# A two-layer hybrid encoder on one core: the later modulation and second norm held until the gates are done, one modulation tile per part on the tensor engine, three weights not kept in the scratch

## The chip, the core and the metric

The kernel runs on one core of a Trainium2 chip. The metric is the time of one execution on the device, in microseconds (us). The core has a tensor engine (PE, with its weight loads listed as PEld), a vector engine (DVE), a scalar engine (ACT), a general engine (POOL) and a queue engine (SP) that issues all of this kernel's transfers in the order in which they were written. Each engine works through its own list of instructions and waits on semaphores for the others.

## The reference

A sequence of 1024 tokens of width 1024 goes through two layers. Each layer normalizes, modulates with a vector made from the condition `c`, mixes, and adds the gated result to the residual.

```python
cond = jax.nn.silu(c)
for i in range(DEPTH):
    mod = cond @ ada_w[i] + ada_b[i]
    shift, scale, gate = jnp.split(mod[:, None, :], 3, axis=-1)
    h = rmsnorm(x, norm_w[i]) * (1 + scale) + shift
    ...
    x = x + gate * y
return rmsnorm(x, final_norm_w)
```

Layer 0 is a gated DeltaNet: 8 query/key heads and 16 value heads of 128, a causal convolution over four tokens, a decay per head and a triangular inverse per chunk. Layer 1 is softmax attention with a forget gate and 16 heads of 64. The modulation is a product of one row of 1024 numbers with a 1024x3072 matrix per layer: shift, scale and gate are 1024 columns each.

## The kernel before

Layer 0 is computed in two halves of 512 tokens. In each half the input projection is made in eight groups (two value heads each), one 128-column tile after the other: a tile is 24 matmuls of 128x512, because every operand is split into a high and a low part (`split`, L321: ACT casts the high part, DVE or POOL subtracts for the low part) and three products are summed. Group by group the keys are transposed (`tr`), their products are taken (`su`), the triangular blocks are inverted on DVE by 15 small steps (`xtmp`, `xi`, L1065 and L1069), merged on PE (`su<-rmat`), and the state runs through `ch` and `co`. Layer 1 follows from about 1300 us.

The order of PE's instructions is fixed by the kernel itself: a small planner (`Flow`, L87) steps through generators by priority and by estimated PE time. On DVE, ACT, POOL and SP a scheduler of the framework sorts the instructions by its own estimate, so that an edit in one place can move instructions in others.

The parts that the change touches:

- **The first modulation** (`start_norm`, L526). Shift (`scol`) and scale (`gcol`) of layer 0 are the two parts of a loop over `n`. In each, eight tiles of 128x1024 of `ada_w` come in through the buffers `og`, `zg`, `d`, `gb`. Tiles 0 to 5 (`KPE` is 6, L81) are multiplied and summed on DVE (L553, L555) into one tile, also called `d`; PE then sums that tile over its partitions with eight matmuls against `ones`, and takes tiles 6 and 7 with eight matmuls each against `cond`. DVE adds the bias into `scol` or `gcol` (L569). With both, ACT and DVE modulate the normalized x into `ht_h` and `ht_l` (L577 to L582), the moving operands of all projections.
- **The later modulation** (`ada_all`, L1174, which calls `ada_strip`, L257). Layer 0's gate and all of layer 1 are made in 16 strips of 256 columns. A strip has eight loads of 128 KB into three buffers `oraw` (L265) and eight DVE steps into `ohi` (L270, L272), then one or two small matmuls and a copy (`olo`, L299). Three small DVE copies from `scol[0]` into the `oraw` buffers (L1177) make the first loads wait for `scol`.
- **The second norm** (`next_norm`, L607). The tokens of the second half are normalized tile by tile: a load into `nx` (L612), a square sum on ACT into `nh` (L305), a scaling on DVE (L594), transposes and modulation, a store to `h1_d`. Nothing holds the first load of `nx`.
- **The gates** (`gates`, L639) of a half: a short projection, a chain of small DVE steps, the running sum `g_gc` of the log decay, its negative `g_ngc` (L686), and a store `g_d` (L696). From `g_d` each group reads a broadcast `gb` twice through one buffer (`decay`, L831): once for `d1`, which goes into the blocks that are inverted (stored as `lb`, read back as `lr`), once for `d2`. After `gb`, POOL masks (L840) and ACT takes the exponential (L852).
- **The scratch of weights** (`proj_src`, L392, and `proj_tile`, L710). In the first half every projection weight is loaded raw into a `wlo` buffer, split, and both parts are stored to `wc` in DRAM (L719); in the second half the two parts are loaded from there (L398), and nothing is split.

Of the kernel before, what the change touches and what calls it, by code (L numbers as in the profile page):

```python
# [15 lines left out]
P = 128  # L16
D = 1024
S = 1024
KT = D // P
# [58 lines left out]
OGW = 2000  # L78
OL = 4
Y_NN = 8000  # L80
KPE = 6  # L81
Y_GA = 14000
Y_N2 = 6000
ADP = 2000
# [97 lines left out]
def tile_trunk(  # L182
# [24 lines left out]
    nc = tc.nc  # L207
# [7 lines left out]
    def ct(shape, name, dt=F32):  # L215
        return const.tile(shape, dt, name=name, tag=name)
# [31 lines left out]
    scol = [ct([P, KT], f"scol{l}") for l in range(2)]  # L248
# [101 lines left out]
    def xt_(shape, name, bufs=1, dt=F32):  # L350
        return px.tile(shape, dt, name=name, tag=name, bufs=bufs)
# [30 lines left out]
    def wtile(n):  # L382
        hi = xt_([P, D], "whi", 3, F32R)
        if "raw" in where:
            raw = where["raw"].pop(0)
            where["raw"].append(raw)
        else:
            raw = xt_([P, D], "wlo", 5)
        lo = xt_([P, D], "wlo", 5, F32R)
        return hi[:, 0:n], lo[:, 0:n], raw[:, 0:n]  # L390

    def proj_src(src, key, again):  # L392
        def load():
            if again:
                hi = xt_([P, D], "whi", 3, F32R)
                lo = xt_([P, D], "wlo", 5, F32R)
                for v, d in zip((hi, lo), wcache[key]):
                    nc.sync.dma_start(v.bitcast(F32), d)  # L398
                return [tuple(v.rearrange("p (k f) -> p k f", f=P) for v in (hi, lo)) + (None,)]
            hi, lo, raw = (v.rearrange("p (k f) -> p k f", f=P) for v in wtile(D))  # L400
            nc.sync.dma_start(raw, src)
            for c in range(2):
                kc = slice(4 * c, 4 * c + 4)
                later.append(lambda kc=kc: split(hi[:, kc], lo[:, kc], raw[:, kc], lo_eng=nc.vector))
            return [(hi, lo, key)]

        return load

# [82 lines left out]
    with ExitStack() as sa:  # L491
# [3 lines left out]
        def at(shape, name, bufs=1, dt=F32):  # L495
            return pa.tile(shape, dt, name=name, tag=name, bufs=bufs)
# [29 lines left out]
        def start_norm():  # L526
            xsT = [at([P, HALF], n, b) for n, b in (("k", KQ), ("k", KQ), ("k", KQ), ("q", 2), ("q", 2))]
            xsT += [at([P, HALF], "ktok", 3) for _ in range(3)]
            for t in range(CPH):
                xt = at([P, D], *(("vtok", 3), ("qd", 2))[t // 2])  # L530
                nc.sync.dma_start(xt, x[t * P : (t + 1) * P, :])
                for d in norm_tile(xt, at([P, D], "ogt", 1), lambda k, p, t=t: nc.scalar.copy(
                    xsT[k][:, t * P : (t + 1) * P], p)):
                    flow.t += d
            tags = [("d1", 2), ("og", 2), ("zg", ZG), ("d1", 2), ("og", 2), ("zg", ZG), ("gb", 1)]
            cnt = [0]

            def wtag():
                cnt[0] += 1
                return tags[cnt[0] % len(tags)]  # L540

            banks = []
            for _ in range(2):
                banks.append((yield from acc_bank()))
            bcol = at([P, 2, KT], "bcol")
            for n in range(2):
                ps = banks[n]
                acc = at([P, D], "d2", 2)
                for k in range(KT):
                    w = at([P, D], *wtag())  # L550
                    nc.sync.dma_start(w, ada_w[0, k * P : (k + 1) * P, n * D : n * D + D])
                    if k == 0:
                        nc.vector.tensor_scalar(acc, w, cond[:, 0:1], None, op0=ALU.mult)  # L553
                    elif k < KPE:
                        nc.vector.scalar_tensor_tensor(  # L555
                            acc, w, cond[:, k : k + 1], acc, op0=ALU.mult, op1=ALU.add
                        )
                    for s, c, on in ((acc, ones[:, 0:1], k == KPE), (w, cond[:, k : k + 1], k >= KPE)):
                        for j in range(KT if on else 0):
                            mm(  # L560
                                ps[:, j : j + 1], s[:, j * P : (j + 1) * P], c,
                                start=s is acc and j == 0, stop=k == KT - 1 and j == KT - 1,
                            )
                if n == 0:
                    nc.sync.dma_start(bcol, ada_bc)
                    nc.sync.dma_start(norm_c, norm_col)
                    wload()
                    wload()
                nc.vector.tensor_tensor((scol, gcol)[n][0], ps[:, 0:KT], bcol[:, n], op=ALU.add)  # L569
                flow.free(ps, R_AD)  # L570
            nc.vector.scalar_tensor_tensor(
                gcol[0], gcol[0], 1.0, norm_c[:, 0], op0=ALU.add, op1=ALU.mult
            )
            for k in range(KT):
                xk = xsT[k]
                sc, sh = gcol[0][:, k : k + 1], scol[0][:, k : k + 1]
                nc.scalar.activation(ht_h[:, k], xk, AF.Identity, scale=sc, bias=sh)  # L577
                if k % 2:
                    nc.scalar.activation(xk, xk, AF.Identity, scale=sc, bias=sh)
                else:  # L580
                    nc.vector.tensor_scalar(xk, xk, sc, sh, op0=ALU.mult, op1=ALU.add)
                nc.vector.tensor_tensor(ht_l[:, k], xk, ht_h[:, k].bitcast(F32), op=ALU.subtract)  # L582
            nc.sync.dma_start(conv_h, conv_col)
            nc.vector.tensor_scalar(conv_h, conv_h, 0.5, None, op0=ALU.mult)
            nc.sync.dma_start(nw_h, a_nw)
            nc.vector.tensor_scalar(nw_h, nw_h, 0.5, None, op0=ALU.mult)
            nc.sync.dma_start(dt_b, a_dt.broadcast_to([P, 16]))
            nc.sync.dma_start(neg_a, a_log.broadcast_to([P, 16]))
            nc.scalar.activation(neg_a, neg_a, AF.Exp)
            nc.vector.tensor_scalar(neg_a, neg_a, -1.0, None, op0=ALU.mult)  # L590
# [16 lines left out]
        def next_norm():  # L607
            yield from hold(lambda: done["kqv"] >= 2)
            for t in range(CPH):
                tok = CPH * P + t * P  # L610
                xt = at([P, D], "nx", 1)
                nc.sync.dma_start(xt, x[tok : tok + P, :])  # L612
                yield 4000
                hf = at([P, KT, P], "nh", 1)

                def evac(k, p):
                    nc.vector.tensor_scalar(
                        hf[:, k], p, gcol[0][:, k : k + 1], scol[0][:, k : k + 1],
                        op0=ALU.mult, op1=ALU.add,
                    )  # L620

                yield from norm_tile(xt, hf.rearrange("p k t -> p (k t)"), evac)
                yield 3000
                nc.sync.dma_start(
                    h1_d[:, :, t * P : (t + 1) * P].rearrange("k p t -> p k t"), hf
                )
            done["norm"] = 1
# [82 lines left out]
        def proj_tile():  # L710
            hi, lo, key = wnext(2)
            ps = yield from acc_bank()
            for k in range(KT):
                if k == 2 and key is not None:
                    wcache[key] = [
                        dram.tile([P, D], F32, name=f"wc{key}{n}", tag=f"wc{key}{n}") for n in range(2)
                    ]
                    for v, d in zip((hi, lo), wcache[key]):
                        nc.sync.dma_start(d.rearrange("p (k f) -> p k f", f=P), v.bitcast(F32))  # L719
                mm3(ps, hi[:, k], lo[:, k], ht_h[:, k], ht_l[:, k], k == 0, k == KT - 1)  # L720
                if k == 1:
                    wload()
                if k in (3, 5):
                    half()
                if k < KT - 1:
                    yield 0
            return ps
# [446 lines left out]
        def ada_all():  # L1174
            yield from hold(lambda: done["gates"] == 1)
            for _ in range(3):
                nc.vector.tensor_copy(xt_([P, 2 * P], "oraw", 3)[:, 0:KT], scol[0])  # L1177
            for l, cl in strips:
                for w0 in (0, 256):
                    yield from ada_strip(  # L1180
                        xt_, acc_bank, l, cl + w0, 256, ("oraw", 3), ("ohi", 4), ("olo", 4), 1, ADP
                    )

        ts = []
# [634 lines left out]
```

## Time and profile before

| what | value |
|---|---|
| time, median of 3 runs | 2058.69 us (2054.26 to 2058.92) |
| the profiled execution | 2063.72 us, its span 2062.0 us |
| PE, PEld busy | 1853.8 us (90%), 1549.9 us (75%) |
| DVE, ACT, POOL busy | 1364.0, 1033.1, 476.4 us |
| HBM read, written | 235.34 MB, 84.81 MB |
| chain that ended last | PE 57%, DMA 16%, DVE 14% |

In the lines of the profile a group reads "line engine operation out<-in, shapes, count | busy us, mean ns of one | idle time of the engine before them, and what ended it". A row of the timeline has the start, the time until the last of its instructions ends, the engine, the line and the operation; in square brackets stands how long the engine had been idle and who released it. SPq is the time in which the queue engine issues a transfer, not the transfer itself. A table of windows gives each engine's busy time in a stretch, then the granted clock of PE (1.00 is full), the share of the DMA engines and GB/s.

### The profile page before, as it was taken

The page shows a single profiled execution, that of the slowest core. Times are in us where ns is not written, and L with a number is a line of the kernel's source. Part 1 is how long each engine was busy: PE and PEld are TensorE (multiplying, and loading weights), DVE is VectorE, ACT ScalarE, POOL GpSimd, SP SyncE. Part 2 cuts the span into 40 slices and gives each one's busy share as a digit, 9 for nine tenths or more (in the row PEclk, how much of TensorE's full clock was granted, in tenths as well). Part 3 has the DMA queues.
Part 4 walks back from the last instruction along what each step waited for, and adds up shares of the span by engine and source line. Part 5 has one row for each costly group of instructions (what it writes and reads, how often), then busy time and mean ns, then how long its engine had stood idle before and what let it go on. Part 6 is the DMA issues. An engine that isn't in the chain of part 4 may idle for free.

```text
span 2062.0 us, 36440 instructions
## 1 busy us (share of the span) xinstructions
PE 1853.8 (90%) x12972; PEld 1549.9 (75%) x12972; DVE 1364.0 (66%) x3310; ACT 1033.1 (50%) x2678; POOL 476.4 (23%) x518
## 2 busy tenths in 40 slices
PE   5867898988998889989989788999999999999898
PEld 5655676767776677778778566879889889889676
DVE  5867888778767567665666476537656566666664
ACT  3554565554545345554444343336555565555631
POOL 2021221211213122212101231421231331331222
PEclk7888999999999999999999999999999999999999
DMA  8767676667655545454459998310211110111522
GB/s 320 255 194 219 192 248 205 202 211 238 198 164 178 154 133 176 128 177 140 145 172 311 323 317 274 108 53 27 67 45 33 57 57 32 57 59 40 170 84 95
DMA packets 238166, 322.55 MB, mean 156 GB/s; under 512 B 103896, under 2 KB 156656, under 8 KB 237984
## 3 DMA queue, kind: packets, MB, share of 16 engines
q1 hardware_dynamic: 237984, 320.22, 48.4%
q8 instruction: 102, 1.67, 0.3%
q14 instruction: 80, 0.66, 0.1%
HBM read 235.34 MB, written 84.81 MB: 155 GB/s over the span
## 4 chain that ended last, share of the span: by engine, by line
PE 57%; DMA 16%; DVE 14%; ACT 5%; issue 3%; POOL 3%; SPq 2%; DVEq 0%; POOLq 0%; ACTq 0%
PE mm L127 36%; PE lg L127 5%; PE pt L131 3%; PE oT L127 3%; DMA oraw<-in_ada_w_dram 3%; PE su L127 2%; PE tr L131 2%; PE co L127 2%; DMA rmat<-rb 2%; DVE wlo L326 2%; DMA ohi<-og_d 2%; PE ch L127 2%; DVE cv_y L743 1%; DMA gb<-g_d 1%; DVE xtmp L1065 1%
## 5 line engine op out<-in xcount | busy, mean ns | idle before, releaser
L127 PE MATMUL mm<-ht_h,whi 128*128 128x512 f32 x784 | 352.1, 449 | 8.8 <-DVE olo L299 6.2
L127 PE MATMUL mm<-ht_l,whi 128*128 128x512 f32 x784 | 317.2, 405 | 5.7 <-DVE ht_l L582 5.7
L127 PE MATMUL mm<-ht_h,wlo 128*128 128x512 f32 x784 | 317.5, 405 | 0.9 <-POOL wlo L326 0.9
L127 PE MATMUL mm<-whi,h_h 128*128 128x384 f32 x512 | 187.3, 366 | 1.7 <-ACT whi L323 1.7
L127 PEld LDWEIGHTS mm<-ht_h,whi 128*128 128x128 f32 x784 | 155.0, 198 | 40.3 <-DVE olo L299 6.7
L127 PEld LDWEIGHTS mm<-ht_h,wlo 128*128 128x128 f32 x784 | 153.4, 196 | 37.0 <-POOL wlo L326 1.3
L127 PEld LDWEIGHTS mm<-ht_l,whi 128*128 128x128 f32 x784 | 154.9, 198 | 32.6 <-DVE ht_l L582 6.9
L127 PE MATMUL mm<-wlo,h_h 128*128 128x384 f32 x512 | 174.1, 340 | 2.7 <-POOL wlo L326 2.7
L743 DVE SCALAR_TENSOR_TENSOR cv_y<-cv_t,conv_h,cv_y 128x512 f32<-128x512 f32 x192 | 146.5, 764 | 42.7 <-ACT cv_y L735 40.4
L127 PE MATMUL mm<-whi,h_l 128*128 128x384 f32 x512 | 173.6, 339 | 0.0
L1559 DVE TENSOR_TENSOR ptl<-pt,pth 128x512 fp32r<-128x512 f32 x192 | 106.3, 555 | 85.0 <-ACT pth L1558 83.3
L1558 ACT CAST pth<-pt 128x512 fp32r<-128x512 f32 x192 | 91.3, 477 | 130.5 <-PE pt L131 129.4
L1402 POOL TENSOR_TENSOR rs<-ss,mhalf 128x4 f32<-128x4 f32 x64 | 64.5, 1007 | 313.3 <-DVE ss L1400 310.6
L1523 ACT ACTIVATE lg<-lg,mx 128x896 f32<-128x896 f32 (+7 forms) x128 | 99.5, 777 | 54.1 <-DVE mx L1515 49.8
L326 DVE TENSOR_TENSOR wlo<-ht_h,whi 128x512 fp32r<-128x512 f32 x124 | 92.3, 785 | 49.9 <-ACT whi L323 44.0
L323 ACT CAST whi<-ht_h 128x512 fp32r<-128x512 f32 x124 | 70.5, 619 | 91.4 <-DMA ht_h<-in_wa_o_dram 37.4
L127 PEld LDWEIGHTS mm<-wlo,h_h 128*128 128x128 f32 x512 | 97.9, 191 | 6.3 <-POOL wlo L326 4.4
L127 PEld LDWEIGHTS mm<-whi,h_h 128*128 128x128 f32 x512 | 98.5, 192 | 4.4 <-ACT whi L323 2.0
L127 PE MATMUL mm<-h_h,whi 128*128 128x512 f32 x240 | 100.4, 419 | 0.6 <-DVE wlo L1658 0.3
L131 PE MATMUL pt<-ident,lg 128*128 128x128 f32 (+1 forms) x584 | 96.6, 275 | 2.8 <-ACT lg L1523 2.8
L127 PEld LDWEIGHTS mm<-whi,h_l 128*128 128x128 f32 x512 | 97.2, 190 | 0.0
L127 PE MATMUL mm<-h_h,wlo 128*128 128x512 f32 x240 | 94.8, 395 | 0.0
(356 smaller groups left out, 4660.6 us busy)
## 6 DMA issues: line engine op xcount, KB each, us to landing
ht_h<-in_wa_o_dram SPq DMA_DIRECT2D x62, 512.0 KB
wc<-whi SPq DMA_DIRECT2D x48, 512.0 KB
wc<-wlo SPq DMA_DIRECT2D x48, 512.0 KB
wlo<-wc SPq DMA_DIRECT2D x48, 512.0 KB
whi<-wc SPq DMA_DIRECT2D x48, 512.0 KB
wlo<-in_wa_c_dram SPq DMA_DIRECT2D x32, 512.0 KB
oraw<-in_ada_w_dram SPq DMA_DIRECT2D x128, 128.0 KB
gb<-g_d SPq DMA_DIRECT2D x32, 512.0 KB
```

Of the source, the lines that this page charges most:

```text
L127: self.nc.tensor.matmul(out, lhsT, rhs, start=start, stop=stop)
L131: self.nc.tensor.transpose(out, src, ident)
L323: nc.scalar.copy(hi, src)
L326: (lo_eng or nc.gpsimd).tensor_tensor(lo, src, hi.bitcast(F32), op=ALU.subtract)
L743: nc.vector.scalar_tensor_tensor(y, raw[:, j : j + HALF], w[:, j : j + 1], y, op0=ALU.mult, op1=ALU.add)
L1065: nc.vector.tensor_tensor(tv, bc(lr[:, j + 1 :, j], 1, m), xi[:, 0:m, j : j + 1].broadcast_to([P, m, n]), op=ALU.mult,)
L1402: nc.gpsimd.tensor_tensor(rs, ss, mhalf[:, 0:4], op=ALU.pow)
L1523: nc.scalar.activation(lg, lg, AF.Exp, scale=-1.0, bias=mx[:, hh : hh + 1], accum_out=sums[:, tt : tt + 1],)
L1558: nc.scalar.copy(ph_[:, cs], pp[:, cs])
L1559: nc.vector.tensor_tensor(pl_[:, cs], pp[:, cs], ph_[:, cs].bitcast(F32), op=ALU.subtract)
```

## The change

The first tile of the first modulation that goes to PE directly is tile 7 instead of tile 6: DVE sums seven tiles, PE takes the sum and one tile. The loads of the strips and the first load of `nx` are held by small DVE copies from `ngc` of the first half's gates. The three weights with keys 0, 1 and 2 (the key, query and first value tile of group 0) are not stored to the scratch; in the second half they are loaded raw and split again.

```diff
-KPE = 6
+KPE = 7
+KC = 3
...
     def proj_src(src, key, again):
         def load():
-            if again:
+            if again and key >= KC:
...
-            return [(hi, lo, key)]
+            return [(hi, lo, None if again else key)]
...
                             mm(
                                 ps[:, j : j + 1], s[:, j * P : (j + 1) * P], c,
-                                start=s is acc and j == 0, stop=k == KT - 1 and j == KT - 1,
+                                start=s is acc and j == 0, stop=s is w and k == KT - 1 and j == KT - 1,
                             )
...
                 xt = at([P, D], "nx", 1)
+                if t == 0:
+                    nc.vector.tensor_copy(xt[:, 0:KT], ts[0]["gt"]["ngc"][:, 0, 0:KT])
                 nc.sync.dma_start(xt, x[tok : tok + P, :])
...
-                if k == 2 and key is not None:
+                if k == 2 and key is not None and key >= KC:
...
             for _ in range(3):
-                nc.vector.tensor_copy(xt_([P, 2 * P], "oraw", 3)[:, 0:KT], scol[0])
+                nc.vector.tensor_copy(xt_([P, 2 * P], "oraw", 3)[:, 0:KT], ts[0]["gt"]["ngc"][:, 0, 0:KT])
```

PE's list is the same as before but for two sets of eight matmuls (tile 6 of each part), which are gone. The other engines' lists are sorted anew; line numbers of the changed kernel are higher by 1 to 3.

On DVE, right after the scale (`gcol`) is complete, the rows of before are these; `ohi` rows are strips, `ht_l` and the rows with `gcol,scol` make the low part of the modulated x:

```order
L571 SCALAR_TENSOR_TENSOR gcol_88<-gcol_88,norm_c 128x8
L272 SCALAR_TENSOR_TENSOR ohi<-oraw,cond,ohi 128x256 x2
L581 TENSOR_SCALAR k<-k,gcol_88,scol_90 128x512
L272 SCALAR_TENSOR_TENSOR ohi<-oraw,cond,ohi 128x256
L582 TENSOR_TENSOR ht_l<-k,ht_h 128x512
L272 SCALAR_TENSOR_TENSOR ohi<-oraw,cond,ohi 128x256
L581 TENSOR_SCALAR k<-k,gcol_88,scol_90 128x512
L272 SCALAR_TENSOR_TENSOR ohi<-oraw,cond,ohi 128x256
```

In the changed kernel the same place on DVE reads:

```order
L572 SCALAR_TENSOR_TENSOR gcol_88<-gcol_88,norm_c 128x8
L582 TENSOR_SCALAR k<-k,gcol_88,scol_90 128x512
L583 TENSOR_TENSOR ht_l<-k,ht_h 128x512
L582 TENSOR_SCALAR k<-k,gcol_88,scol_90 128x512
L583 TENSOR_TENSOR ht_l<-k,ht_h 128x512
L582 TENSOR_SCALAR q<-q,gcol_88,scol_90 128x512
```

No strip stands between the rows that modulate x any more; the strips begin behind `g_ngc`.

On ACT, at the first group's keys, before has these rows; `sqt` are square sums of the transposed keys and queries, `ktok` is the copy that frees the transposes' bank, `d` with `g_gc` is the exponential of `d1`, `d` with `g_ngc` that of `d2`, which reads the second `gb`:

```order
L898 ACTIVATE sqt,gss<-tr 128x128
L852 ACTIVATE d_757<-d_757,g_gc 128x128 x8
L898 ACTIVATE sqt,gss<-tr 128x128
L747 ACTIVATE cv_t<-cv_y 128x512
L852 ACTIVATE d_872<-d_872,g_ngc 128x128 x3
L928 ACTIVATE gb<-gb 128x512
L852 ACTIVATE d_872<-d_872,g_ngc 128x128
L928 ACTIVATE gb<-gb 128x512
L852 ACTIVATE d_872<-d_872,g_ngc 128x128 x4
L898 ACTIVATE sqt,gss<-tr 128x128 x2
L902 COPY ktok<-tr 128x512
```

The changed kernel has them on ACT in this order:

```order
L901 ACTIVATE sqt,gss<-tr 128x128
L855 ACTIVATE d_731<-d_731,g_gc 128x128 x8
L901 ACTIVATE sqt,gss<-tr 128x128 x3
L905 COPY ktok<-tr 128x512
L750 ACTIVATE cv_t<-cv_y 128x512
L901 ACTIVATE sqt,gss<-tr 128x128 x2
L905 COPY vtok<-tr 128x4x128
L901 ACTIVATE sqt,gss<-tr 128x128 x2
L905 COPY vtok<-tr 128x4x128
L855 ACTIVATE d_846<-d_846,g_ngc 128x128 x3
```

The copy `ktok` has moved from behind the exponentials of `d2` to a place ahead of them.

On SP, from the store of the gates to the reload of the first group's blocks, before has these rows:

```order
L696 DMA g_d<-cv_t 16x512
L401 DMA wlo<-in_wa_z_dram 128x1024
L834 DMA gb<-g_d 128x1024
L719 DMA wc_1190<-whi 128x1024
L719 DMA wc_1191<-wlo 128x1024
L834 DMA gb<-g_d 128x1024
L401 DMA wlo<-in_wa_z_dram 128x1024
L719 DMA wc_1253<-whi 128x1024
L719 DMA wc_1254<-wlo 128x1024
L834 DMA gb<-g_d 128x1024 x2
L1051 DMA lb<-d_757 32x8x32 x4
L1055 DMA lr_890<-lb 32x16x16 x4
```

In the changed kernel SP has, from the same store on, up to the same blocks (`lb`):

```order
L699 DMA g_d<-cv_t 16x512
L615 DMA nx<-in_x_dram 128x1024
L402 DMA wlo<-in_wa_z_dram 128x1024
L266 DMA oraw<-in_ada_w_dram 128x256
L837 DMA gb<-g_d 128x1024
L266 DMA oraw<-in_ada_w_dram 128x256
L722 DMA wc_1164<-whi 128x1024
L722 DMA wc_1165<-wlo 128x1024
L266 DMA oraw<-in_ada_w_dram 128x256 x2
L402 DMA wlo<-in_wa_z_dram 128x1024
L722 DMA wc_1228<-whi 128x1024
L837 DMA gb<-g_d 128x1024
```

Seven strip loads, three of them just ahead of `g_d`, now stand among the gates' transfers up to the second `gb`. Behind it come one more store of a weight, three strip loads, and then `lb`, which no longer stands behind the third and fourth `gb`.

## The prediction

> **What bounds the kernel now.** First the table of windows, to see where PE is short of work.
>
> ```profile
> 0.00:52.00 52.00, 27.83 (x128) 26.00 (x128) 28.46 (x50) 16.77 (x51) 14.35 (x30) 0.70 0.88 320
> 52.00:62.00 10.00, 3.89 (x7) 2.28 (x8) 9.64 (x21) 8.13 (x12) 0.00 (x0) 0.50 0.41 123
> 100.00:130.00 30.00, 14.92 (x78) 11.78 (x76) 11.80 (x31) 22.14 (x73) 14.65 (x17) 0.77 0.51 159
> 130.00:200.00 70.00, 52.52 (x506) 41.80 (x507) 56.27 (x159) 29.49 (x70) 10.29 (x18) 0.87 0.78 243
> 200.00:300.00 100.00, 89.14 (x825) 71.66 (x825) 84.03 (x220) 59.98 (x185) 27.18 (x32) 0.97 0.65 208
> 1300.00:1500.00 200.00, 193.71 (x1115) 170.15 (x1114) 115.56 (x317) 99.32 (x221) 59.85 (x55) 0.98 0.17 53
> ```
>
> The first number behind each stretch is its length, the next PE's busy time. From 1300 us on PE is busy 97%, at 200 to 300 us 89%: there time is PE's work, and a shift made earlier is carried. In the first 62 us PE is busy 31.7 us, from 100 to 200 us 67.4 of 100. The change acts there. Second, PE's waits over the whole span:
>
> ```profile
> PE su L127 <- DMA rmat<-rb: 22.1, 4, 10.3
> PE tr L131 <- ACT ktok L902: 12.5, 1, 12.5
> PE mm L127 <- DVE d L555: 9.7, 2, 6.2
> PE mm L127 <- DVE olo L299: 6.2, 1, 6.2
> PE mm L127 <- DVE ht_l L582: 5.7, 2, 4.2
> ```
>
> All five lie in or begin in the first 200 us (the 10.3 of `rmat` too), so I follow the change through that stretch on the timeline.
>
> **Step A, the two parts of the first modulation.**
>
> ```profile
> 26.91 0.75 DVE L553 TENSOR_SCALAR d<-zg,cond 128x1024 f32<-128x1024 f32 x1 [2.63 <-DMA zg<-in_ada_w_dram]
> 38.14 1.29 DVE L555 SCALAR_TENSOR_TENSOR d<-d,cond,d 128x1024 f32<-128x1024 f32 x1 [0.61 <-DMA d<-in_ada_w_dram]
> 39.48 3.57 PE L127 MATMUL mm<-ones,d 128*128 128x1 f32 x16 [6.22 <-DVE d L555]
> 42.91 3.55 PE L127 MATMUL mm<-cond,og 128*128 128x1 f32 x16
> 46.33 3.55 PE L127 MATMUL mm<-cond,zg 128*128 128x1 f32 x16
> 51.12 0.15 DVE L569 TENSOR_TENSOR gcol<-mm,bcol 128x8 f32<-128x8 f32 x1
> 25.00:30.00 5.00, 5.00 (x25) 5.00 (x25) 2.05 (x3) 0.00 (x0) 0.00 (x0) 0.50 1.00 374
> 35.00:40.00 5.00, 0.52 (x3) 0.52 (x3) 3.78 (x5) 0.46 (x1) 0.00 (x0) 0.50 1.03 410
> ```
>
> Per part a tile costs PE 46.33 - 42.91 = 3.42 us and one more DVE step 1.29: on this chain 3.42 - 1.29 = 2.1 us less. The first part's gain only lets buffers go earlier; the second part's sets `gcol`. PE's last product ended at 46.33 + 3.55 = 49.9, but DVE, deep in strips, took the sum only at 51.12: 1.2 us that go with the strips. And the chain is paced by transfers (both DVE rows above waited for one, with all DMA engines busy at 374 to 410 GB/s). Ahead of the last tiles 1.5 MB leave the queue: the load of `nx` and the two stores of the first weight, 0.5 MB each (128x1024 numbers of 4 bytes); at 0.4 MB per us that is 3.7 us at most, nothing at least. I take 2.9, near the top, since the rows do wait for DMA; tile 6 of part two, whose buffer PE frees, then lands about 36.5. Sum A: 2.1 + 1.2 + 2.9 = 6.2 (3.3 to 7.0), `gcol` at 44.9.
>
> The Trainium skill (TensorE: Matmul & The Clock Gate, Part 1) says that PE runs at full clock once it has been busy for some 3.4 us. By that rule a tile would soon cost PE half, 1.7 us, and the tile's 2.1 would shrink to 0.4. The trace disagrees for these one-column products: busy throughout 25 to 30 us, the granted clock stayed at 0.50.
>
> **Step B, modulating x.**
>
> ```profile
> 51.56 2.22 ACT L577 ACTIVATE ht_h<-k,scol,gcol 128x512 fp32r<-128x512 f32 x3 [7.03 <-DVE gcol L571]
> 57.22 0.80 ACT L579 ACTIVATE k<-k,scol,gcol 128x512 f32<-128x512 f32 x1
> 59.81 0.68 DVE L582 TENSOR_TENSOR ht_l<-k,ht_h 128x512 fp32r<-128x512 f32 x1
> 60.55 0.80 PE L127 MATMUL mm<-ht_l,whi 128*128 128x512 f32 x1 [4.18 <-DVE ht_l L582]
> ```
>
> From 60.55 on PE runs without a stop. It waits for the second `ht_l`, which needs ACT until 57.22 + 0.80 = 58.0 and one DVE step of 0.68; DVE began it 1.8 us late, behind strips. With no strips there, 1.8 us go (1 to 2). PE resumes 8.0 us earlier, at 52.5. Both later weights are ready by then: their loads stand ahead in the queue.
>
> **Step C, the first keys.**
>
> ```profile
> 97.42 0.32 SPq L834 DMA_DIRECT2D gb<-g_d  x1
> 103.26 1.46 POOL L840 TENSOR_SCALAR_AFFINE_SELECT d<-gb 128x1024 f32<-128x1024 f32 x1 [4.13 <-DMA gb<-g_d]
> 104.75 2.44 ACT L852 ACTIVATE d<-d,g_gc 128x128 f32<-128x128 f32 x8
> 111.36 0.99 ACT L852 ACTIVATE d<-d,g_ngc 128x128 f32<-128x128 f32 x3 [3.20 <-POOL d L840]
> 115.40 0.58 ACT L902 COPY ktok<-tr 128x512 f32<-128x512 f32 x1
> 116.03 1.11 PE L131 MATMUL tr<-ident,vt 128*128 128x128 f32 x4 [12.48 <-ACT ktok L902]
> ```
>
> The longest stall: ACT does `d2` (second `gb`) ahead of `ktok`. In the new order `ktok` follows `d1` and three square sums: 104.75 + 2.44 + 3 x 0.4 + 0.6 = 109.0 instead of 116.0, 7 us. Against it stand the strips: three loads are queued ahead of `g_d`, and the first `gb` stands behind a load that waits for the first strip step on DVE. I put that at 2.4 us (bounds 0.3, one issue, and 5, a load's landing as in `gb`), and 1.5 us for the second transposes, which now wait for ACT's square sums of the queries. ACT also meets `nx` here; a late `nx` holds it up to 3 us, mostly while it would wait for `gb`. Gain 7.0 - 2.4 - 1.5 = 3.1 (-2 to 7). Total 11.1.
>
> **Step D, the bank held by `olo`.**
>
> ```profile
> 115.46 5.14 SPq L834 DMA_DIRECT2D gb<-g_d  x2
> 120.69 1.86 SPq L1051 DMA_DIRECT2D lb<-d  x4
> 128.85 0.69 DVE L1065 TENSOR_TENSOR xtmp<-lr,xi 128x15 f32<-128x15 f32 x1 [1.87 <-DMA lr<-lb]
> 133.54 0.40 DVE L299 COPY olo<-mm 1x256 f32<-1x256 f32 x1
> 134.00 0.79 PE L127 MATMUL mm<-ht_h,whi 128*128 128x512 f32 x1 [6.25 <-DVE olo L299]
> ```
>
> `lb` stood 5.1 us behind two `gb`; now it stands ahead of them. With `d1` done by 106.5 (ktok's sums, POOL's power of 1 us, 2.2 us of products), `lb` goes at 106.6, the blocks are back 8.2 us later (128.85 - 120.69), at 114.8, and `olo` follows 4.7 us behind: 119.9 for PE instead of 134.0, 14.1 in all, so D gives 3.0 (0 to 6).
>
> **Step E, what the strips take back.**
>
> ```profile
> L272 DVE SCALAR_TENSOR_TENSOR ohi<-oraw,cond,ohi 128x256 f32<-128x256 f32 x28 | 14.2, 506 | 9.5 <-DMA oraw<-in_ada_w_dram 8.9
> sum 120.60, PE 94.62 PEld 75.41 DVE 96.33 ACT 59.10 POOL 22.46; mean PE 31.54 PEld 25.14 DVE 32.11 ACT 19.70 POOL 7.49
> ```
>
> Of the strips' steps 32 lay ahead of the first inversion step, now 12 do: 20 x 0.506 = 10.1 us of DVE move into the stretch from there to the third group's last step (128.8 to 249.4 before, the sum row), where DVE had 120.6 - 96.3 = 24.3 us idle. If all fits, it costs nothing, if nothing fits, 10. In the new list the second group's inversion passes twelve strip steps, four convolutions and eight `nh` steps, which speaks for little. I take 3. PE's list puts the strips' matmuls where they were; only the first is near its strip.
>
> **Step F, the second half.**
>
> ```profile
> 588.59 0.42 DVE L971 TENSOR_TENSOR ve<-ch,g_ex 128x256 f32<-128x256 f32 x1 [8.23 <-ACT vn L970]
> 545.42 0.68 DVE L326 TENSOR_TENSOR wlo<-wlo,whi 128x512 fp32r<-128x512 f32 x1
> 544.28 1.14 ACT L323 CAST whi<-wlo 128x512 fp32r<-128x512 f32 x2 [0.17 <-PE mm L127]
> ```
>
> Three weights are split again: 3 x 1.14 = 3.4 us of ACT and 6 x 0.68 = 4.1 of DVE around 540 to 600, where DVE has a hole of 8.2 us. Zero; four DVE steps stand ahead of the last inversion step there, so 2.7 at most. Three loads fewer there, and 3 MB of stores less early, are in A.
>
> **Sum.** 6.2 + 1.8 + 3.1 + 3.0 - 3 - 0 = 11.1 us of the profiled execution's 2063.72, so 2052.6. The median of the runs stands 0.24% below that execution (2058.69); scaled, 2047.6.
>
> **Rivals.** (1) *The gain ends with the start.* DVE is full where the strips go (84% at 200 to 300 us): E costs the 10.1. Then 14.1 - 10.1 = 4.0, 2054.7. For it: DVE's chains end most of PE's later waits. Against: 24 us idle. (2) *More than I take.* E costs nothing and the second group's `rmat` wait (10.3) halves, since its DVE work comes earlier: 14.1 + 5 = 19.1, 2039.6. (3) *Slower: strip loads block the queue.*
>
> ```profile
> 47.26 20.27 SPq L265 DMA_DIRECT2D oraw<-in_ada_w_dram  x21
> ```
>
> A load whose buffer is not yet free holds all behind it: 0.97 us each here. Until the second group's `rmat` load 35 of them now stand behind `g_d` where 16 stood; 19 x 0.97 = 18.4 if each holds a `gb`, `lb` or `rmat` load on PE's path, against A and B: 8.0 - 18.4, slower by 10.4, 2069.1. It decides once that `rmat` lands later than 196.7. For it: `gb` stands right behind strip loads; against: a DVE that is less loaded frees buffers in time. The Trainium skill (DMA: Bandwidth & Descriptors, Anatomy of one DMA) has the waits sit in the issuing sequencer; by that rule, and by the row, this mechanism is real, only its size is open.
>
> **Chances and range.** Forecast 0.53 (2041 to 2053), more 0.14, rival (1) 0.16, slower 0.15 (the row of the queue shows its mechanism at work already), else 0.02. The bounds of the steps sum to wider ends, but do not fall together; the range 2036 to 2060 takes in the first three but for the tail of the second. 0.3% (6.2 us) is about what a measurement tells from no change. Faster by more: the first two and the lower edge of (1), 0.70; within 0.15; slower 0.15.
>
> **What would show it.** `gcol` near 45 and PE unbroken from 52 to 53 (A, B); `ktok` at 102 to 104 and PE's stall there 8 us (C); `lb` near 107 and `olo` near 120 (D); `rmat` merges at 153 and 181 to 185 instead of 163.6 and 196.7 (E); no new PE wait from 540 to 620 (F). I am wrong if `gb` lands later than 100, or if PE's waits from 140 to 300 grow by 8 us.

## The result, and the profile of the changed kernel

The changed kernel takes 2044.16 us (median of 7 runs, 2039.24 to 2048.92) where the kernel before takes 2058.92 (7 runs, 2051.98 to 2063.17): a ratio of 0.9929, 95% interval 0.9908 to 0.9951, 14.8 us faster by the medians. The forecast was 2047.6, in a range of 2036 to 2060. Its profiled execution has a span of 2044.3 us against 2062.0. The runs of one kernel spread by 10 us and more, so a single profile's end says less than its beginning; how much less, experiment 10 shows. One execution of experiment 7 (3555.57 us) and one of experiment 11 (3725.38 us) took far longer than the rest and are left out of their ratios.

First the table of windows of the changed kernel, for the stretches that were shown of before (length, busy time of PE, PEld, DVE, ACT and POOL, granted clock, DMA share, GB/s):

```profile
0.00:52.00 52.00, 23.72 (x100) 20.56 (x100) 28.86 (x44) 20.80 (x56) 13.49 (x29) 0.70 0.66 242
52.00:62.00 10.00, 8.16 (x26) 6.63 (x27) 4.30 (x7) 4.50 (x8) 0.00 (x0) 0.67 0.02 4
100.00:130.00 30.00, 21.10 (x81) 16.56 (x82) 24.14 (x63) 19.98 (x67) 13.74 (x16) 0.72 0.68 203
130.00:200.00 70.00, 58.63 (x674) 45.29 (x673) 62.24 (x164) 33.51 (x87) 16.12 (x18) 0.93 0.81 261
200.00:300.00 100.00, 87.40 (x670) 69.89 (x669) 85.00 (x229) 56.58 (x174) 27.18 (x32) 0.93 0.70 226
1300.00:1500.00 200.00, 193.22 (x1131) 169.19 (x1130) 120.07 (x332) 105.87 (x237) 53.14 (x47) 0.98 0.14 44
```

PE is busy 8.16 of the 10 us from 52 on (3.89 before), 21.10 from 100 to 130 us (14.92) and 58.63 from 130 to 200 us (52.52). DVE's share from 130 to 200 us has grown from 56.27 to 62.24 us: the strips are there now. Next PE's waits over the whole span, the rows that answer to the five of before:

```profile
PE mm L128 <- DVE d L556: 13.6, 2, 8.6
PE su L128 <- DMA rmat<-rb: 9.3, 2, 7.7
PE mm L128 <- DVE olo L300: 8.0, 3, 5.0
PE tr L132 <- ACT ktok L905: 6.4, 1, 6.4
PE mm L128 <- DVE ht_l L583: 3.9, 2, 3.4
```

The wait for `ktok` has about halved (12.5 before), that for `rmat` fell from 22.1 to 9.3 us; PE waits longer for the sum `d` (13.6 against 9.7), since DVE makes more of it. Then the timeline at the steps of the prediction, start and first keys:

```profile
37.77 1.28 DVE L556 SCALAR_TENSOR_TENSOR d<-og,cond,d 128x1024 f32<-128x1024 f32 x1 [0.68 <-DMA og<-in_ada_w_dram]
42.54 3.55 PE L128 MATMUL mm<-cond,zg 128*128 128x1 f32 x16
46.13 0.17 DVE L570 TENSOR_TENSOR gcol<-mm,bcol 128x8 f32<-128x8 f32 x1 [7.08 <-PE mm L128]
53.84 0.80 PE L128 MATMUL mm<-ht_l,whi 128*128 128x512 f32 x1 [3.42 <-DVE ht_l L583]
99.22 2.45 ACT L855 ACTIVATE d<-d,g_gc 128x128 f32<-128x128 f32 x8 [1.06 <-POOL d L843]
102.62 0.58 ACT L905 COPY ktok<-tr 128x512 f32<-128x512 f32 x1
103.25 1.12 PE L132 MATMUL tr<-ident,vt 128*128 128x128 f32 x4 [6.41 <-ACT ktok L905]
105.05 1.11 PE L132 MATMUL tr<-ident,vt 128*128 128x128 f32 x4 [0.68 <-ACT vtok L905]
107.77 1.82 SPq L1054 DMA_DIRECT2D lb<-d  x4
121.36 0.79 PE L128 MATMUL mm<-ht_h,whi 128*128 128x512 f32 x1 [4.97 <-DVE olo L300]
157.60 0.39 PE L128 MATMUL su<-rmat,d 32*16 32x16 f32 x4 [7.66 <-DMA rmat<-rb]
182.37 0.21 PE L128 MATMUL su<-rmat,d 32*16 32x16 f32 x2
```

DVE takes `gcol`'s sum the moment PE's last product is there (42.54 + 3.55 = 46.1). PE's second wait for `ht_l` ends at 53.84 (60.55 before), the copy `ktok` starts at 102.62 (115.40), the second transposes start at 105.05 (117.49), the blocks leave at 107.77 (120.69), and `olo` releases PE at 121.36 (134.00). But the first merges start only at 157.60: of a lead of 12.6 us, 6.0 are left there (163.62 before).

For all kernels below I use the **lead**: the time at which PE starts a product in the first profile of before, less the time at which it starts the same product here. The products are named by their time in before.

| kernel | 76 | 118 | 149 | 197 | 278 | 647 | 688 | 1383 | 1916 |
|---|---|---|---|---|---|---|---|---|---|
| before, second profile (10) | 0.1 | 0.6 | 0.7 | 0.8 | 0.8 | 7.2 | 7.3 | 10.3 | 9.9 |
| changed | 6.7 | 12.4 | 11.5 | 14.4 | 6.1 | 12.7 | 17.8 | 16.7 | 17.6 |
| changed, second profile (9) | 7.5 | 13.3 | 12.9 | 16.1 | 9.7 | 13.4 | 18.7 | 21.5 | 20.0 |
| seven tiles alone (1) | -0.4 | -0.7 | -1.6 | -0.4 | -1.8 | 9.9 | 10.8 | 10.3 | 10.9 |
| strips held alone (2) | 1.6 | 5.7 | 6.1 | 1.9 | -0.4 | 5.1 | 6.1 | 1.2 | 2.3 |
| nx held alone (3) | -1.3 | 4.4 | 6.1 | 4.9 | 5.2 | 9.4 | 10.9 | 12.2 | 12.3 |
| three weights alone (4) | -0.6 | 0.4 | 0.8 | 2.0 | 0.1 | 2.5 | 4.8 | -3.3 | -3.1 |
| six tiles again (5) | 6.0 | 10.7 | 13.1 | -0.7 | 1.1 | 2.6 | 6.9 | 5.8 | 7.0 |
| strips not held (6) | 2.2 | 7.1 | 8.5 | 8.3 | 3.5 | 8.8 | 12.6 | 9.5 | 8.0 |
| nx not held (7) | 6.4 | 10.8 | 12.7 | 3.2 | 0.4 | 7.1 | 12.0 | 15.6 | 14.1 |
| all weights stored (8) | 5.1 | 11.0 | 12.8 | 8.1 | 6.1 | 10.2 | 12.1 | 11.9 | 12.1 |
| two steps a strip (11) | 7.0 | 12.7 | 18.4 | 11.6 | 11.6 | 12.3 | 20.4 | 20.1 | 20.8 |
| one load a strip (12) | 7.6 | 13.2 | 13.1 | 4.8 | 7.5 | 22.0 | 29.5 | 24.6 | 26.6 |

### The profile page after: what moved, and what is told of

Same layout as the page of the kernel before. It is cut to its first block, busy times and chain, and to the rows that moved or that the text cites. A ratio compares the mean times of both kernels' runs of the same rounds, so it can differ in the third digit from the quotient of the medians.

```text
span 2044.3 us, 36353 instructions
## 1 busy us (share of the span) xinstructions
PE 1852.2 (91%) x12940; PEld 1546.6 (76%) x12940; DVE 1378.0 (67%) x3319; ACT 1036.5 (51%) x2684; POOL 484.5 (24%) x518
## 4 chain that ended last, share of the span: by engine, by line
PE 54%; DVE 16%; DMA 16%; ACT 5%; issue 4%; SPq 3%; POOL 2%; DVEq 0%; POOLq 0%; ACTq 0%
PE mm L128 35%; PE lg L128 5%; PE pt L132 3%; PE oT L128 3%; DVE wlo L327 2%; PE tr L132 2%; PE co L128 2%; PE su L128 2%; DMA lr<-lb 2%; DMA wraw<-in_wb_dram 2%; DMA oraw<-in_ada_w_dram 2%; DVE cv_y L746 2%; DVE xtmp L1068 1%; DVE d L887 1%; DVE xi L1072 1%
## 5 line engine op out<-in xcount | busy, mean ns | idle before, releaser
L327 DVE TENSOR_TENSOR wlo<-ht_h,whi 128x512 fp32r<-128x512 f32 x124 | 94.1, 802 | 52.9 <-ACT whi L324 46.5
L324 ACT CAST whi<-ht_h 128x512 fp32r<-128x512 f32 x124 | 70.6, 619 | 103.7 <-DMA ht_h<-in_wa_o_dram 34.1
L324 ACT CAST whi<-wlo 128x512 fp32r<-128x512 f32 (+1 forms) x108 | 62.6, 626 | 72.8 <-PE mm L128 34.4
```

The lines of the kernel that those rows point to most:

```text
L324: nc.scalar.copy(hi, src)
L327: (lo_eng or nc.gpsimd).tensor_tensor(lo, src, hi.bitcast(F32), op=ALU.subtract)
```

## The experiments

My theory was P: the gain is made on the path of the start, part by part, and is kept. The rival was S: each edit re-sorts the lists of DVE, ACT, POOL and SP for the whole program, and the time is mostly decided by how later waits fall.

### 1 to 4: each edit alone, on the kernel before

**1, seven tiles.**

```diff
-KPE = 6
+KPE = 7
```

> Only the first edit: seven tiles on DVE, one on PE; strips, nx and the scratch as before. Theory P (the gain is made on the path of the start, part by part, and is kept): 2.1 us of PE products go from the chain to gcol; nothing else there changes, so gcol near 49, PE's last gap near 58.5, and the copy of the first keys still behind the second group of exponentials. Time lower than before by about 2 us, 2057, too little to be told from no change. Theory S (every edit re-sorts the lists of DVE, ACT, POOL and SP for the whole program, and the time is mostly decided where waits fall later, after 280 us): the shift at 60 us says nothing of the end; the time differs from before by 5 us or more either way, and the difference arises after 130 us.

Measured: ratio 0.9994 (0.9976 to 1.0012), no change. `gcol` is complete at 50.39 us (51.12 before), PE's last gap ends at 60.73 (60.55): nothing at the start.

**2, the hold of the strips.**

```diff
-nc.vector.tensor_copy(xt_([P, 2 * P], "oraw", 3)[:, 0:KT], scol[0])
+nc.vector.tensor_copy(xt_([P, 2 * P], "oraw", 3)[:, 0:KT], ts[0]["gt"]["ngc"][:, 0, 0:KT])
```

> Only the hold of the strips. Theory P: DVE takes gcol's sum at once (1.2 us) and modulates x without strips between (1.8 us), and the copy of the first keys is made ahead of the second exponentials (some 6 us less of that stall); strips come back on DVE between 130 and 280 us and take 6 us. PE's last gap near 57, a shift of 9 to 10 at 117 us, 3 to 4 at 280 us, and a time about 4 us under before, 2055. Theory S: the shift at 280 us is not the end's; what follows 280 us adds or takes 5 us or more.

Measured: 1.0012 (0.9999 to 1.0025). The gap ends at 58.31 and the lead is 5.7 at 118 us, where P expected 57 and 9 to 10; all of it is lost again by 278 us (-0.4), where P expected 3 to 4 left.

**3, the hold of nx.**

```diff
+if t == 0:
+    nc.vector.tensor_copy(xt[:, 0:KT], ts[0]["gt"]["ngc"][:, 0, 0:KT])
```

> Only the hold of the first load of nx (0.5 MB less ahead of the tiles of the first modulation). Theory P: 1.3 us at most off gcol (0.5 MB at 0.4 MB per us); the copy of the first keys now stands ahead of the second exponentials, with no strips' loads in front of the gates' store, so 5 to 7 us off that stall, kept at 280 us since strips stay early: about 2052. Theory S: as above, the shift at 280 us is not the end's.

Measured: 0.9977 (0.9964 to 0.9991), 5 us faster. Nothing is gained at the start (`gcol` at 51.93); as P expects, PE's stall at the first keys falls from 12.48 to 6.74 us, and a lead of 5.2 us is left at 278 us.

**4, three weights not stored.**

```diff
+KC = 3
-            if again:
+            if again and key >= KC:
-                if k == 2 and key is not None:
+                if k == 2 and key is not None and key >= KC:
```

> Only the three weights that are not stored and are split again in the second half. Theory P: 1.0 MB less ahead of the last tiles, 2 us off gcol at most, the stall at the first keys as before; in the second half 3.4 us of ACT and 4.1 of DVE near 540 to 600 us under PE's work, no new wait there: 2057. Rival Q (the stores crowd the queue all through the first half, and without them weights arrive earlier there): 5 us or more by 500 us. Theory S: a change of 5 us or more that arises after 280 us and has nothing to do with stores.

Measured: 1.0048 (1.0033 to 1.0062), 10 us slower, which neither P nor the rival on stores forecast; of the three only S leaves room for it. Up to 1000 us its profile has leads between -2.0 and 8.3 us, and -3.3 at 1383.

The four ratios less 1 add up to -0.0006 + 0.0012 - 0.0023 + 0.0048 = +0.0031, 6 us slower; together the edits give -0.0071. They do not add, so P in its simple form falls. Why not at the start, DVE's timeline of the fourth kernel shows:

```profile
45.74 0.49 DVE L273 SCALAR_TENSOR_TENSOR ohi<-oraw,cond,ohi 128x256 f32<-128x256 f32 x1 [1.22 <-DMA oraw<-in_ada_w_dram]
48.26 0.48 DVE L273 SCALAR_TENSOR_TENSOR ohi<-oraw,cond,ohi 128x256 f32<-128x256 f32 x1 [2.03 <-DMA oraw<-in_ada_w_dram]
50.98 1.00 DVE L273 SCALAR_TENSOR_TENSOR ohi<-oraw,cond,ohi 128x256 f32<-128x256 f32 x2 [1.26 <-DMA oraw<-in_ada_w_dram]
51.91 0.16 DVE L570 TENSOR_TENSOR gcol<-mm,bcol 128x8 f32<-128x8 f32 x1
44.89 3.55 PE L128 MATMUL mm<-cond,zg 128*128 128x1 f32 x16
```

PE's last product ends at 44.89 + 3.55 = 48.4, yet DVE takes the sum at 51.91: ahead of it in DVE's list stand strip steps that wait for their own loads. While the strips are early, whatever PE or the tiles gain waits there; without the strips, tiles and products set the time. The start is a maximum of chains, not a sum. I called that theory M.

### 5 to 8: each edit undone, on the changed kernel

**5, six tiles again** (`KPE = 6`).

> The changed kernel with six tiles on DVE and two on PE again; the other three edits stay. Theory M (at the start three things run side by side, PE's products, the tiles' transfers and DVE's strips, and only the last of them sets gcol, so one edit alone gains little and one edit undone costs its own term in full): gcol later than the changed kernel's 46.1 by 2 us (3.42 of PE less 1.29 of DVE), that is 48, and the time 2 us above the changed kernel's, ratio to before 0.994. Theory S (late waits fall by the order of the lists, whatever the start does): a ratio that is not explained by the shift at 62 us.

Measured: 0.9987 (0.9969 to 1.0005). `gcol` comes at 46.73, only 0.6 us later than in the changed kernel, and PE's gap ends at 54.44. The rows tell why not 2:

```profile
34.96 1.28 DVE L556 SCALAR_TENSOR_TENSOR d<-d,cond,d 128x1024 f32<-128x1024 f32 x1
46.73 0.17 DVE L570 TENSOR_TENSOR gcol<-mm,bcol 128x8 f32<-128x8 f32 x1 [10.49 <-PE mm L128]
```

With six tiles DVE's sum is done at 34.96 + 1.28 = 36.2, in the changed kernel at 37.77 + 1.28 = 39.1, 2.8 us later: the seventh step itself takes 1.28, it waits 0.68 for its tile to land, and the steps ahead of it start some 0.8 us later (the step on `gb` at 33.28 against 32.55), because the third of them now stands behind the sum of the shift. DVE's part costs 2.8 us, not 1.29, against 3.42 of PE: 0.6 is left. The time nevertheless grows by 0.58% (from 0.9929 to 0.9987), 12 us and not the 2 that M expected, and the lead falls to -0.7 at 197 us: it is lost at the merges, below.

**6, strips held only until the shift is done** (`scol[0]` in the copies).

> The changed kernel with the strips' first loads held only until the shift is done, as before; seven tiles, nx held, three weights not stored. Theory M: gcol's sum on DVE again stands behind strips that wait for transfers, gcol at 50 to 51 and PE's last gap near 58 to 59, 5 us later than the changed kernel's 53.8; the copy of the first keys still ahead of the second exponentials (6 us stay); no strips come back on DVE from 130 to 280 us (5 to 6 us less there). Time about that of the changed kernel, ratio 0.993. Rival H (the hold is what the change lives on, its gain at the start is kept): 6 us or more above the changed kernel, ratio 0.996 or more. Theory S: not explained by the shifts at 62 and 280 us.

Measured: 0.9969 (0.9950 to 0.9987). `gcol` 49.81, gap to 59.12: the start loses 5.3 us, as M expects. DVE again, and PE's last product:

```profile
46.76 1.00 DVE L273 SCALAR_TENSOR_TENSOR ohi<-oraw,cond,ohi 128x256 f32<-128x256 f32 x2 [1.64 <-DMA oraw<-in_ada_w_dram]
49.41 0.48 DVE L273 SCALAR_TENSOR_TENSOR ohi<-oraw,cond,ohi 128x256 f32<-128x256 f32 x1 [1.06 <-DMA oraw<-in_ada_w_dram]
49.81 0.16 DVE L570 TENSOR_TENSOR gcol<-mm,bcol 128x8 f32<-128x8 f32 x1
42.93 3.55 PE L128 MATMUL mm<-cond,zg 128*128 128x1 f32 x16
```

The product is there at 46.5, and DVE comes 3.3 us late. The ratio is the one that rival H gave, 8 us above the changed kernel, and that the strips then cost nothing from 130 to 280 us is not borne out: the lead goes from 8.5 to 3.5.

**7, nx not held.**

> The changed kernel with the first load of nx unheld. Theory M: 0.5 MB more ahead of the tiles, 1.3 us at most on gcol; 1 us above the changed kernel, ratio 0.9935. Theory S: a difference of 4 us or more that arises after 130 us.

Measured: 0.9966 (0.9947 to 0.9986). The start is as in the changed kernel (`gcol` 45.77, gap to 53.48): the 0.5 MB of `nx` cost it nothing. The lead is lost at the merges (12.7 at 149, 3.2 at 197, 0.4 at 278 us), as S expects.

**8, all weights stored** (`KC = 0`).

> The changed kernel with all weights stored to the scratch and none split twice. Theory M: 1.0 MB more ahead of the last tiles, 2 to 2.5 us on gcol; in the second half nothing to be seen or, if the edit alone cost 10 us by its second splits, up to 10 us less there. Ratio 0.994 by the start alone; 0.990 or less if the second splits cost 10 us wherever they stand. Theory S: neither, with the difference arising where no weight is stored or split.

Measured: 0.9985 (0.9968 to 1.0002), 11 us above the changed kernel, where the same edit alone had cost 10. `gcol` 47.61, gap to 55.31: 1.5 us at the start, near M's 2 to 2.5. At 197 us it is 6.3 behind the changed kernel, at 278 us level with it (6.1 both). M's ratio of 0.994, or less, is missed.

### Where the lead goes: the inversions

In the four kernels of 5 to 8 PE's gap at the start ends 1.4 to 7.1 us earlier than before (60.55), and at 278 us they lead by 0.4 to 6.1. The first steps of the first group's inversion, the two issues of its inverted blocks `rb` (first and second group) and PE's longest wait for the merges up to 300 us:

| kernel | first step | rb, first group | length | other DVE steps in it | rb, second group | PE's wait |
|---|---|---|---|---|---|---|
| before | 128.85 | 153.15 | 24.3 | 36 | 188.26 | 10.3 |
| changed | 116.37 | 146.25 | 29.9 | 44 | 171.15 | 7.7 |
| changed, second profile | 115.14 | 144.83 | 29.7 | 44 | 169.38 | 7.6 |
| six tiles again (5) | 116.25 | 150.35 | 34.1 | 54 | 171.31 | 17.0 |
| strips not held (6) | 122.03 | 153.82 | 31.8 | 51 | 168.06 | 11.6 |
| nx not held (7) | 118.55 | 157.52 | 39.0 | 63 | 173.65 | 16.1 |
| all weights stored (8) | 115.33 | 142.05 | 26.7 | 40 | 183.74 | 13.1 |

An inversion is 15 pairs of steps on DVE. Its length grows with the number of other steps that DVE's list puts between them. The windows of both inversions, before and then changed:

```profile
128.85:153.15 24.30, 19.15 (x84) 15.74 (x85) 21.55 (x66) 9.85 (x25) 1.22 (x5) 0.86 0.77 236
153.15:188.26 35.11, 31.11 (x356) 24.05 (x354) 31.86 (x88) 18.49 (x43) 8.49 (x13) 0.95 0.87 272
```

```profile
116.37:146.25 29.88, 24.91 (x109) 20.41 (x109) 28.39 (x74) 18.06 (x46) 16.97 (x13) 0.89 0.83 258
146.25:171.15 24.90, 16.46 (x213) 12.07 (x211) 22.54 (x73) 8.89 (x21) 1.58 (x5) 0.79 0.75 232
```

DVE is the third engine column: 21.55 of 24.30 and 28.39 of 29.88 us, so it is nearly full; the first inversion became 5.6 us longer, the second 10.2 shorter. The groups of DVE work within the first inversion of the changed kernel, and of the one that leaves `nx` unheld:

```profile
L273 DVE SCALAR_TENSOR_TENSOR ohi<-oraw,cond,ohi 128x256 f32<-128x256 f32 x10 | 5.8, 580 | 1.1 <-DMA oraw<-in_ada_w_dram 1.1
L746 DVE SCALAR_TENSOR_TENSOR cv_y<-cv_t,conv_h,cv_y 128x512 f32<-128x512 f32 x6 | 4.4, 734 | 0.0
```

```profile
L744 DVE SCALAR_TENSOR_TENSOR cv_y<-cv_t,conv_h,cv_y 128x512 f32<-128x512 f32 x9 | 6.6, 738 | 0.0
L273 DVE SCALAR_TENSOR_TENSOR ohi<-oraw,cond,ohi 128x256 f32<-128x256 f32 x14 | 6.6, 473 | 3.2 <-DMA oraw<-in_ada_w_dram 3.2
L618 DVE TENSOR_SCALAR nh<-tr,gcol,scol 128x128 f32<-128x128 f32 x8 | 2.8, 392 | 0.0
```

Unheld, `nx` brings eight scalings `nh`, three convolution steps and four strip steps more into that inversion, 39.0 us long. Before had seven strip steps there:

```profile
L272 DVE SCALAR_TENSOR_TENSOR ohi<-oraw,cond,ohi 128x256 f32<-128x256 f32 x7 | 3.3, 475 | 1.7 <-DMA oraw<-in_ada_w_dram 1.7
```

Three more strip steps alone do not make up the 5.6 us. The thirty steps of the inversion also take longer themselves, 9.4 us in the changed kernel and 6.0 in before. A step of 0.2 us takes over 1 us where POOL is at work on a mask (`d<-gb`) or on `qd`:

```profile
117.49 1.09 POOL L843 TENSOR_SCALAR_AFFINE_SELECT d<-gb 128x1024 f32<-128x1024 f32 x1 [2.95 <-DMA gb<-g_d]
117.53 1.08 DVE L1072 TENSOR_TENSOR xi<-xi,xtmp 128x26 f32<-128x26 f32 x1
125.08 2.53 POOL L932 TENSOR_TENSOR qd<-q,gb 128x512 f32<-128x512 f32 x2 [1.49 <-ACT gb L931]
125.23 1.19 DVE L1068 TENSOR_TENSOR xtmp<-lr,xi 128x36 f32<-128x36 f32 x1
126.34 1.55 DVE L273 SCALAR_TENSOR_TENSOR ohi<-oraw,cond,ohi 128x256 f32<-128x256 f32 x1
```

In before this POOL work was nearly done (at 129.5 us) when the first inversion began at 128.85. The earlier start puts the inversion beside it; no experiment separates this from the longer list.

The second merges give 8.4 us back (lead 6.0 at the first merges, 14.4 at 197 us), since before's wait of 10.3 us is gone. By 278 us they are lost again: for the same products from 197 to 278 us PE is idle 13.4 us instead of 9.6, and busy 75.8 instead of 71.2 at a lower granted clock (0.94 against 0.97). From the first merges to 278 us both kernels need 113.9 us. No experiment was aimed at this stretch.

### 9 and 10: both kernels once more

> The changed kernel once more, unaltered. If the four kernels with one edit undone (ratios 0.9966 to 0.9987) are really slower than it, its ratio comes out at 0.993 again; if they only look slower because it was timed at another time, at 0.995 to 0.998. The second profile tells which late differences are the order's and which are one execution's luck: by the order (theory M with S) the waits near 157, 680 and 870 us are again within 1 to 2 us of the first profile's; by luck they differ by 4 us or more.

Measured: 0.9923 (0.9903 to 0.9944). This interval lies below those of the four kernels with one edit undone, so the changed kernel is faster than each of them. Its second profile differs from the first by 1.5 us at most up to 149 us, by 5.1 at most up to 278 and by 2.4 at 1916; the waits near 157 us (7.6 and 7.7), near 670 (0.3 and 1.6) and near 870 us (under 1.3 in both) agree.

> The kernel before once more, for a second profile. By the order: the waits for rmat near 196 and 687 us (10.3 and 9.1 us) and for the value tokens near 640 us (8.5) are there again. By luck: they move by 4 us or more, and with them the shift from the first profile after 300 us.

Measured: a single time of 2052.88 us, and a second profile, span 2051.2. Up to 278 us the two profiles of before agree within 1.3 us; from 446 us on (2.9) they part, by 7 at 647 and 10 at 1916. The waits at the merges are there again (9.5 near 196 us), that for the value tokens near 640 us is 6.6 instead of 8.5; of the second half's first merges, the rows of before's second profile and of the changed kernel's first:

```profile
680.36 0.31 PE L127 MATMUL su<-rmat,d 32*16 32x16 f32 x4 [8.94 <-DMA rmat<-rb]
```

```profile
669.84 0.30 PE L128 MATMUL su<-rmat,d 32*16 32x16 f32 x4 [1.63 <-DMA rmat<-rb]
```

So what differs before 300 us by more than these few us, and the wait at 688, belongs to the order of the lists; much else after 400 us is one execution's luck, of up to 12 us, and in the single profiles of experiments 1 to 8 a late difference can't be told from it. Of the theories M holds at the start; at the merges the order of DVE's list decides, which fits S.

### 11 and 12: is it the strips' steps or their loads

**11, two steps a strip.** It leaves six of the eight slices out of each later modulation's sum.

```diff
-                else:
+                elif k == KT - 1:
                     nc.vector.scalar_tensor_tensor(
```

> The changed kernel with two steps on DVE per strip instead of eight (six of the eight 128-row slices of each later modulation are loaded and left out of the sum); all loads stay. Theory D (the first inversion is stretched by strip steps between its own on DVE, 24.3 us before and 29.9 in the changed kernel, and PE waits for the merges): the inversion takes 24 to 26 us, the first merge starts by 153 us, and the shift at 280 us is 10 or more instead of 6. Theory Q (the strips' loads block the queue, and so the round trips of the blocks): inversion and first merge as in the changed kernel, within 2 us.

Measured: the first inversion takes 138.67 - 116.41 = 22.3 us, and the first merges start 10.5 us earlier than in the changed kernel:

```profile
138.67 1.97 SPq L1078 DMA_DIRECT2D rb<-xi  x4
174.38 3.10 SPq L1078 DMA_DIRECT2D rb<-xi  x4
```

The inversion holds 29 other steps instead of 44, and its own steps take 8.0 us instead of 9.4. Theory D holds for that inversion; the lead at 278 us is 11.6, where the changed kernel's two profiles have 6.1 and 9.7. But the second group's `rb` leaves at 174.38, later than the changed kernel's 171.15: its inversion now holds 16 `nh` and nine convolution steps, 35.7 us, and PE waits 13.6 us there. The time is no better: 0.9926 (0.9897 to 0.9955), with 96 steps of DVE fewer.

**12, one load a strip.** Seven eighths of the later modulation's weights are left out.

```diff
+                if kk == 0:
                     w = alloc([P, width], *(wtag() if callable(wtag) else wtag))
                     nc.sync.dma_start(w, ada_w[layer, kk * P : (kk + 1) * P, col : col + width])
```

> The changed kernel with one load per strip instead of eight (all eight steps on DVE read the first slice; seven eighths of the later modulation's weights are left out, 14.7 MB of transfers); all steps on DVE stay. Theory D: the steps are as dense as before, so the inversion stays near 30 us and the first merge near 157. Theory Q: the queue no longer stops at strips' loads, the four rmat loads are issued 4 us behind rb instead of 6.5, the inversion loses its waits, and the shift at 280 us is 10 or more.

Measured: 0.9903 (0.9881 to 0.9926), perhaps 5 us better than the changed kernel (medians 2036.3 and 2041.2 on one chip; the intervals overlap). The first inversion goes from 124.67 to 157.56, 32.9 us, and PE waits 13.8 us: it holds 54 other steps, eight `nh` among them, and the first merges start at 163.8, not near the 157 that D expected. With most loads gone it is no shorter, so theory Q falls for the first group. `rmat` is issued 4.4 us behind `rb` instead of 6.5, as Q expects. What gain there is arises after 300 us.

## Why the prediction was right, and where it was not

The forecast of 2047.6 lies 3.4 us from the time measured; it took off 11.1 us, and 14.8 are measured. By its steps (leads at PE):

- **A and B, the start**: 8.0 expected, 6.7 and 7.5 measured at 76 us. B is right in size: from `gcol` to the end of PE's gap 53.84 - 46.13 = 7.7 us instead of 9.4. A gave 51.1 - 46.1 = 5.0 of 6.2, but its parts were wrong and partly cancel: the tile was put at 2.1 and is worth 0.6 (5), the strips at 1.2 and are worth 3.7 (49.81 - 46.13 in 6), `nx` and stores at 2.9 and are worth 0 and 1.5 (7, 8). The step that failed is costing the moved tile at DVE's 1.29 us: it delays DVE's sum by 2.8, the wait for its landing and the later start of the steps ahead of it included. And as a sum of separate gains the step was wrong: alone, three of the four edits give nothing there (1, 3, 4), since DVE's strips hold `gcol` at 50 to 52 us.
- **C and D**: 6.1 expected together, and 12.4 - 6.7 = 5.7 and 12.6 - 12.4 = 0.2 measured, 5.9. The split was wrong. `ktok` ends at 102.62 + 0.58 + 6.7 = 109.9 on before's scale, where 109.0 was worked out without strips: their loads in front of the gates' transfers cost 0.9 us, not 2.4. The second transposes follow `ktok` by 2.4 us instead of 2.1, so they lose 0.3, not 1.5. D's 3.0 were the other side of that: with C larger nothing was left for it, and `olo` came at 121.4 instead of 119.9 with the 1.3 us that A lacked. PE's stall at the keys fell to 6.4 us, where 8 was expected. No single edit was needed for the order on ACT; the hold of `nx` alone and that of the strips alone both bring it (4.4 and 5.7 at 118 us).
- **E**: -3 expected, -6.5 and -4.2 measured from the product at 134 us to 278 us (12.6 to 6.1; 13.9 to 9.7). The prediction weighed DVE's idle time and the second group's inversion, which became 10.2 us shorter; the loss came at the first, which it did not price. That strip steps among its steps lengthen it is borne out by 11; POOL's work beside it is a second cause that the rows show and no experiment separates. The first merges came at 157.6 and 156.1, not at 153, the second at 182.4 and 180.6, inside 181 to 185 or next to it. What I also did not weigh is how much the outcome hangs on the list: in 5 and 7 the same early start is swallowed whole.
- **F**: 0 expected. In the changed kernel PE waits 1.6 and 1.7 us for split weights between 560 and 570 us; the kernel of 8, which splits none twice, has 0.9 and 1.7 there. So the splits are hidden but for some 0.7 us, but the second half's first merges gave some 5 us (lead 12.7 to 17.8, and 13.4 to 18.7) which no step held. There before's wait of 9.1 us for `rmat` became 1.6. The prediction had counted it among waits of the first 200 us: it is part of the 22.1 in its first row. The five rows that it showed were also not the five longest; `vtok` with 17.8 and `ve` with 15.4 us stood above most of them.

At 278 us the forecast stood at 11.1, and the mean of two profiles each is (6.1 + 9.7 - 0.8) / 2 = 7.5. So about half of the measured gain was made where I placed it; the total came out close by luck: two misses have opposite signs, an E that was too small and a gain in the second half that no step held. Of the rivals, (1) had 4.0 at that point, at a price of 10.1 for the strips that was not reached. Of (2) one half came true: the wait of 10.3 us before the second merges is gone, but what that gave is lost again by 278 us. (3) is not what happened: the waits for `rmat` fell.

What stays open: how the loss at the first inversion divides between the longer list and POOL's work beside it; which instructions of the later lists make the three-weights edit cost 10 us alone and gain 11 beside the others, and what makes executions of one kernel differ by 10 us after 400 us. The early windows do not hold it, and single profiles cannot tell it from luck.

## What to carry to other kernels

Where several chains meet at one instruction, price an edit by which chain ends last after it, not by the sum of what each edit takes off its own: alone these edits gave +6 us, together -15. Background work that is listed on DVE between the steps of a serial chain became latency here: the first inversion took 22.3 us with 29 other steps in it and 39.0 with 63. The number of foreign steps inside a chain can be read from the order of the list before the run; what another engine does beside it has to be looked for too. Take two profiles of the same kernel before believing a difference late in the span.

## What the runs showed of the hardware that was not expected

That one-column products leave the clock at 0.50 the rows of before had shown, and the changed kernel shows it again (PE busy all of 40 to 45 us). New is how long wide products take to raise it: with 128x512 products without a stop from 53.84 on, one takes 0.63 us until 57.84 and 0.39 from 58.65, so the full clock comes 4.0 to 4.8 us in. This moment is not fixed: over the fourteen profiles the first product of 0.4 us starts 3.0 (6) to 6.1 us (7) after PE's last gap of the start ends, and in the second profile of the changed kernel, with the same list, 3.1 us. The leads of 6.7 and 7.5 at 76 us differ by that.

```profile
40.00:45.00 5.00, 5.00 (x25) 5.00 (x25) 0.00 (x0) 0.00 (x0) 1.66 (x2) 0.50 0.01 3
57.84 0.63 PE L128 MATMUL mm<-ht_l,whi 128*128 128x512 f32 x1
58.65 0.39 PE L128 MATMUL mm<-ht_h,whi 128*128 128x512 f32 x1
```

The Trainium skill (TensorE: Matmul & The Clock Gate, Part 1) names a busy window of about 3.4 us that runs free, so that the moment varies from run to run, by 0.5 us to either side. The wide products agree that it varies, but by more, 3.0 to 6.1 us; that a busy PE comes to the full clock, the one-column products do not show.

Nor was it expected that small DVE steps are held up beside POOL. In the inversions of the first two groups, in the twelve profiles other than those of 1 and 4, the 566 steps `xtmp` and `xi` beside which POOL had no instruction took 0.12 to 0.22 us each; beside POOL's `qd<-q,gb` most took 0.6 to 1.3 us, beside its masks eight of fourteen took 1.05 to 1.11 us. Beside its small `ln_rs` (25 steps) none took over 0.20 us. Which instructions hold each other up is not tested here.
